# Merging the block inverses of both halves of a DeltaNet head together, with one set of decays

## The chip, the cores and the metric

The kernel runs on one core of one Trainium2 chip. The metric is the device time of one execution in microseconds (us). TensorE, VectorE, ScalarE, GpSimd and SyncE appear in the profile as PE, DVE, ACT, POOL and SP; PEld is the load of stationary operands into TensorE, SPq the queue in which SP issues transfers.

## The reference: what is computed

One layer of a decoder with two head groups, for a prompt of 2048 tokens and for 8 single-token samples. The part that matters here is the gated DeltaNet group (4 heads of width 128), computed chunk by chunk:

```python
G = jnp.cumsum(gc, axis=-1)
diff = G[..., :, None] - G[..., None, :]
L = jnp.exp(jnp.where(causal, diff, -jnp.inf))
kb = kc * bc[..., None]
A = jnp.where(strict, jnp.einsum('bhtk,bhsk->bhts', kb, kc) * L, 0.0) + eye
rhs = jnp.concatenate([vc * bc[..., None], kb * jnp.exp(G)[..., None]], axis=-1)
sol = lax.linalg.triangular_solve(A, rhs, left_side=True, lower=True, unit_diagonal=True)
u = sol[..., :V] - jnp.einsum('bhtk,bhkv->bhtv', sol[..., V:], s)
attn = jnp.einsum('bhtk,bhsk->bhts', qc, kc) * L
o = (jnp.einsum('bhtk,bhkv->bhtv', qc * jnp.exp(G)[..., None], s)
     + jnp.einsum('bhts,bhsv->bhtv', attn, u))
```

Around it stand an input projection of width 4104, an HGRN2 group of the same size, gates, norms, and an output projection of 1024 by 1024 with a residual and a final norm.

## The kernel before, in words

The prompt is worked in two groups of 1024 tokens (`g`), each in two halves of 512 tokens (`sb`, four chunks of 128). For each group the four heads follow one another, so there are eight (group, head) pairs, called heads below. Projections run as three products of split operands (`xh`, `xl`, `wh`, `wl`) into `ps_pj`. The recurrences of the heads run as generators beside them. Every operation is recorded by `Engine` (line 392 in all rows; TensorE's products are on line 505, its transposes on line 512), and `Model.plan` sets the order on each engine by a list schedule with a table of costs (`_time`, and `hold` in `mm`). The engines then run that order, so an engine whose next instruction is not ready waits even if a later one is.

For one DeltaNet head:

- `decays` makes, for each half, two masked sets of decays from the gates' cumulated logs: `la` (rows t, columns s, mask `mnA`) and `lt` (rows s, columns t, mask `mnT`), four scalar_tensor_tensor and one Exp each.
- `gk_after` and `gq_after` make the scalars `gam`, `nge`, `br`, the products `ps_kq` of keys with keys and queries, `la` = products times `gam` times `la`, `lt` = products times `lt`. The 32 by 32 diagonal blocks of `la` go through DRAM (`ad`) into `xa`, one block a partition.
- `substitute` inverts all 32 blocks of a head (both halves) at once on DVE: 31 steps of two operations, `tm<-xa,ti` and `ti<-ti,tm`. The result goes through DRAM (`td`) into the diagonal blocks of `ut`, one tile per half, eight transfers a head.
- `inverse`, one generator per half, merges blocks of 32 into 64 and 64 into 128: four groups of small products (`ps_v1`, `ps_u1`, `ps_v2`, `ps_u2`; the profile shows them as `ps_v` and `ps_u` with 32 or 64 columns), each followed by copies on DVE, and a 32 by 32 block transpose of `ut` into `tn`.
- `gdn_chain` walks the chunks: `ps_ks`, `rr`, `ps_u<-rr,ut`, `uu`, `ps_s`, the state `s_gd`, and the output `po_g`.

After the eighth head's projections the output projection (`ps_y`) begins, while the last head's substitution, merge and chain still run.

Of the kernel before, what the change touches and what calls it, by code (L numbers as in the profile page):

```python
# [7 lines left out]
F32 = mybir.dt.float32  # L8
# [9 lines left out]
P = 128  # L18
# [385 lines left out]
def build(tc, x_prompt, x_sample, state_hgrn, state_gdn, state_gdn_conv, norm_w, w_in, hg_lb_logits,  # L404
# [10 lines left out]
    with ctx:  # L415
# [79 lines left out]
        def until(cond):  # L495
            while not cond():
                yield 0.3
# [206 lines left out]
        def gates_post(g, gt, out):  # L704
# [127 lines left out]
        def gk_after(g, h, sb, gt):  # L832
            cs = slice(sb * 4, sb * 4 + 4)

            def run(u):
                yield from until(lambda: "ek" in u)
                ps = yield from tr4(r4(u[1]), "ps_k")
                ss = sumsq4(ps, "ssk")
                V.tensor_scalar(ss, ss, 4 * EPS, None, op0=ALU.add)
                rk = small.tile([P, 4], F32, tag="rk", name="rk")  # L840
                rsqrt(rk, ss)
                kn = keep.tile([P, 4, P], F32, tag="kn", name="kn")
                V.tensor_tensor(kn, ps, bc4(u["ek"]), op=ALU.mult)
                u["kn"] = kn
                yield
                br = small.tile([P, 4], F32, tag="br", bufs=6, name="br")
# [34 lines left out]

        def gq_after(sb, U):
            def run(u):
# [8 lines left out]
                k2, q2 = r4(u[1]), r4(u[0])  # L892
                la, lt, gam = u["la"], u["lt"], u["gam"]
                for c2 in range(2):
# [6 lines left out]
                    for c in range(2):  # L901
                        cc = 2 * c2 + c
                        V.scalar_tensor_tensor(la[:, cc], in0=pk[:, c, 0], scalar=gam[:, cc:cc + 1], in1=la[:, cc], op0=ALU.mult, op1=ALU.mult)
                    V.tensor_tensor(lt[:, 2 * c2:2 * c2 + 2], pk[:, :, 1], lt[:, 2 * c2:2 * c2 + 2], op=ALU.mult)
                for b in range(4):
                    Q.dma_start(U["ad"][b, sb * 4:sb * 4 + 4].rearrange("c t s -> t c s"),
                                      la[32 * b:32 * b + 32, :, 32 * b:32 * b + 32])
# [12 lines left out]
        def substitute(U):  # L920
# [3 lines left out]
            for cg in range(4):  # L924
                Q.dma_start(xa[32 * cg:32 * cg + 32], U["ad"].rearrange("b c t s -> (b c) t s"))
            ti = dec.tile([P, 8, 32], F32, tag="ti", name="ti")
# [16 lines left out]
            for sb in range(NSB):  # L943
                ut = keep.tile([P, 4, P], F32, tag="ut", name="ut")
                G.memset(ut, 0.0)
                for b in range(4):
                    Q.dma_start(ut[32 * b:32 * b + 32, :, 32 * b:32 * b + 32],
                                      td[b, sb * 4:sb * 4 + 4].rearrange("c s t -> s c t"))
                U[sb]["ut0"] = ut
            for sb in range(NSB):  # L950
                start(inverse(U[sb], sb), 0)

        def inverse(u, sb):
            la, ut = u["la"], u["ut0"]
            v1, v2 = v12[sb]
# [3 lines left out]
            yield from ready(la, ut, slot=CH)  # L959
            pv = ch.tile([P, 4, 32], F32, tag="ch", name="ps_v1")  # L960
            for c in range(4):
                for q in (0, 64):
                    mm(pv[q:q + 32, c], lhsT=la[:, c, q:q + 32], rhs=ut[:, c, q + 32:q + 64], start=True, stop=True)
            for q in (0, 64):
                V.tensor_copy(v1[q:q + 32], pv[q:q + 32])
            yield from ready(v1, tn, slot=CH)
            pu = ch.tile([P, 4, 32], F32, tag="ch", name="ps_u1")
            for c in range(4):
                for q in (0, 64):
                    mm(pu[q:q + 32, c], lhsT=tn[:, c, q:q + 32], rhs=v1[:, c], start=True, stop=True)  # L970
                mm(pu[32:64, c], lhsT=v1[:, c], rhs=tn[:, c, 0:32], start=True, stop=True)
            for q in (0, 64):
                V.tensor_scalar(ut[q:q + 32, :, q + 32:q + 64], pu[q:q + 32], -1.0, None, op0=ALU.mult)
            V.tensor_scalar(tn[32:64, :, 0:32], pu[32:64], -1.0, None, op0=ALU.mult)
            yield from ready(ut, slot=CH)
            pv2 = ch.tile([P, 4, 64], F32, tag="ch", name="ps_v2")
            for c in range(4):
                mm(pv2[:64, c], lhsT=la[:, c, 0:64], rhs=ut[:, c, 64:128], start=True, stop=True)
            V.tensor_copy(v2[0:64], pv2[:64])
            yield from ready(v2, tn, slot=CH)  # L980
            pu2 = ch.tile([P, 4, 64], F32, tag="ch", name="ps_u2")
            for c in range(4):
                mm(pu2[:64, c], lhsT=tn[:, c, 0:64], rhs=v2[:, c], start=True, stop=True)
            opened[0] -= 1
            V.tensor_scalar(ut[0:64, :, 64:128], pu2[:64], -1.0, None, op0=ALU.mult)
            u["ut"] = ut

        def gdn_chain(g, h, U, gt):
            S = s_gd[h]
            for sb in range(NSB):  # L990
# [6 lines left out]
                for c in range(4):  # L997
# [506 lines left out]
        for i, (g, h, off, sb, part) in enumerate(steps):  # L1504
# [6 lines left out]
            if i == 7:  # L1511
# [5 lines left out]
                G.affine_select(out=mnT, in_=mnT, compare_op=ALU.is_ge, fill=NEG, base=0, pattern=[[1, P]], channel_multiplier=-1)  # L1517
                mnA = ctile([P, P], "mnA")
                G.memset(mnA, 0.0)
                G.affine_select(out=mnA, in_=mnA, compare_op=ALU.is_gt, fill=NEG, base=0, pattern=[[-1, P]], channel_multiplier=1)  # L1520
                t0 = ctile([P, 8, 32], "t0")
# [6 lines left out]
                for b in range(2):  # L1528
                    G.memset(scT[b], 0.0)
                v12 = [(ctile([P, 4, 32], f"v1{b}"), ctile([P, 4, 64], f"v2{b}")) for b in range(2)]  # L1530
                for t in v12:
                    G.memset(t[0], 0.0)
                    G.memset(t[1], 0.0)
                zpad = ctile([P, NS, 40], "zpad")
# [28 lines left out]
            elif off == GQ:  # L1563
                post = conv_post(0, h, UG[sb], gq_after(sb, UG), lambda u=UG[sb]: "gam" in u)
            elif off == GV:
# [265 lines left out]
```

## Time and profile before

| what | before |
|---|---|
| time, median of 3 runs (lowest, highest) | 1274.28 us (1273.73, 1276.13) |
| the profiled execution: its own time | 1279.08 us |
| the profiled execution: span from first to last instruction | 1277.3 us |
| PE busy | 1220.3 us, 96% of the span |
| DVE busy | 950.4 us, 74% |
| ACT busy | 519.1 us, 41% |
| POOL busy | 306.3 us, 24% |

Busy time is the time in which an engine executed something. A product of four-byte floats shows as two rows per instruction on PE, and rows of PE overlap, since its products are pipelined: the duration of a row is longer than its distance to the next one.

### The profile page before, as it was taken

Reading aid. Unit: us, or ns where it says so; the run is one execution under the profiler, and the core shown is the slowest. Engines: PE = TensorE matmul, PEld = TensorE weight load, DVE = VectorE, ACT = ScalarE, POOL = GpSimd, SP = SyncE. Lnnn points to the kernel's source line nnn. Section 1 sums busy time; section 2 is a strip of 40 time slices with the busy share of each in tenths; the row PEclk is TensorE's granted clock in tenths of the full one; section 3 lists DMA queues with packets and bytes.
Section 4 is the critical chain, followed back from the end, with each engine's and each line's share of the span. In section 5 each row is a group of like instructions: output and inputs, shape, how many; then the busy total and the mean of one; then the engine's idle time right before and its main releaser. Section 6 shows DMA issues by size and latency. Waiting matters only on the chain.

```text
span 1277.3 us, 21956 instructions
## 1 busy us (share of the span) xinstructions
PE 1220.3 (96%) x7943; PEld 1056.3 (83%) x7943; DVE 950.4 (74%) x2419; ACT 519.1 (41%) x1533; POOL 306.3 (24%) x304
## 2 busy tenths in 40 slices
PE   3999999999999999989999999999999999999997
PEld 3988898988898889987788878888887887877785
DVE  4467897689876986888788987896788677954433
ACT  5435523643264325653365326423622464222221
POOL 5221321332232322322224213221322220001000
PEclk9999999999999999999999999999999999999998
DMA  5222532332333321334144432221332216442442
GB/s 177 66 50 85 80 41 58 71 100 64 79 93 86 92 58 42 87 108 111 34 118 57 65 68 69 70 56 30 80 76 49 68 49 202 129 144 83 144 144 82
DMA packets 144053, 107.52 MB, mean 84 GB/s; under 512 B 26122, under 2 KB 126792, under 8 KB 143928
## 3 DMA queue, kind: packets, MB, share of 16 engines
q1 hardware_dynamic: 143936, 106.02, 32.8%
q8 instruction: 65, 1.06, 0.3%
q14 instruction: 52, 0.43, 0.1%
HBM read 82.23 MB, written 23.91 MB: 83 GB/s over the span
## 4 chain that ended last, share of the span: by engine, by line
PE 69%; DVE 15%; DMA 9%; SPq 3%; issue 2%; ACT 1%; POOL 0%; POOLq 0%; DVEq 0%; ACTq 0%
PE ps_pj L505 35%; PE ps_y L505 14%; DVE tm L392 4%; DVE ti L392 4%; SPq L392 3%; PE ps_u L505 2%; PE po_h L505 2%; PE po_g L505 2%; PE ps_kq L505 2%; DMA ut<-td 2%; DMA xt<-in_x_prompt_dram 1%; DVE E L392 1%; PE ps_g L505 1%; PE ps_ks L505 1%; PE ps_hu L505 1%
## 5 line engine op out<-in xcount | busy, mean ns | idle before, releaser
L505 PE MATMUL ps_pj<-xh,wh 128*128 128x512 f32 (+2 forms) x1328 | 469.8, 354 | 7.9 <-ACT pre L392 2.7
L505 PE MATMUL ps_pj<-xh,wl 128*128 128x512 f32 (+2 forms) x1328 | 466.2, 351 | 0.0
L505 PE MATMUL ps_pj<-xl,wh 128*128 128x512 f32 (+2 forms) x1328 | 465.2, 351 | 0.2 <-DVE xl L392 0.2
L505 PEld LDWEIGHTS ps_pj<-xh,wh 128*128 128x128 f32 x1328 | 253.4, 191 | 34.8 <-ACT pre L392 3.3
L505 PEld LDWEIGHTS ps_pj<-xl,wh 128*128 128x128 f32 x1328 | 253.5, 191 | 24.2 <-DVE xl L392 0.5
L505 PEld LDWEIGHTS ps_pj<-xh,wl 128*128 128x128 f32 x1328 | 253.4, 191 | 24.3
L392 POOL TENSOR_TENSOR wl<-raw,wh 128x512 fp32r<-128x512 f32 x128 | 172.9, 1352 | 359.6 <-ACT wh L392 319.9
L392 ACT ACTIVATE wh<-raw 128x512 fp32r<-128x512 f32 x128 | 80.5, 629 | 158.4 <-PE ps_pj L505 111.3
L392 DVE TENSOR_TENSOR tm<-xa,ti 128x248 f32<-128x248 f32 (+30 forms) x248 | 107.5, 434 | 14.6 <-DMA xa<-ad 9.4
L505 PE MATMUL ps_y<-woh,oh 128*128 128x512 f32 x256 | 101.4, 400 | 4.9 <-ACT oh L392 3.0
L505 PE MATMUL ps_y<-woh,ol 128*128 128x512 f32 x256 | 101.0, 396 | 0.0
L505 PE MATMUL ps_y<-wol,oh 128*128 128x512 f32 x256 | 100.4, 394 | 0.0
L392 DVE TENSOR_TENSOR ti<-ti,tm 128x248 f32<-128x248 f32 (+30 forms) x248 | 90.4, 365 | 7.5
L392 ACT ACTIVATE jk<-xt 128x512 bf16<-128x512 f32 (+2 forms) x54 | 40.0, 740 | 121.9 <-DVE xt L392 88.2
L392 POOL TENSOR_TENSOR rso<-sso,mhalf 128x4 f32<-128x4 f32 x32 | 35.8, 1119 | 115.7 <-DVE sso L392 111.5
L505 PEld LDWEIGHTS ps_y<-woh,oh 128*128 128x128 f32 x256 | 48.5, 190 | 15.1 <-ACT oh L392 3.5
L392 POOL TENSOR_TENSOR frs<-fss,mhalf 128x1 f32<-128x1 f32 (+1 forms) x17 | 9.5, 557 | 198.4 <-DVE fss L392 180.9
L505 PEld LDWEIGHTS ps_y<-woh,ol 128*128 128x128 f32 x256 | 48.4, 189 | 10.3 <-DVE ol L392 0.4
L505 PEld LDWEIGHTS ps_y<-wol,oh 128*128 128x128 f32 x256 | 48.6, 190 | 9.4
L392 DVE TENSOR_TENSOR xt<-ps_y,xt 128x512 f32<-128x512 f32 (+1 forms) x34 | 23.4, 688 | 39.4 <-PE ps_y L505 38.0
L392 ACT ACTIVATE s_hg<-s_hg,e 128x128 f32<-128x128 f32 x80 | 32.0, 400 | 43.0 <-DVE s_hg L392 32.3
L392 DVE SCALAR_TENSOR_TENSOR s_gd<-s_gd,el,ps_s 128x128 f32<-128x128 f32 x64 | 22.1, 346 | 30.8 <-PE ps_s L505 30.3
(290 smaller groups left out, 2169.5 us busy)
## 6 DMA issues: line engine op xcount, KB each, us to landing
raw<-in_w_in_dram SPq DMA_DIRECT2D x128, 256.0 KB
xt<-in_x_prompt_dram SPq DMA_DIRECT2D x30, 512.0 KB
og_d<-sz SPq DMA_DIRECT2D x32, 256.0 KB
og<-og_d SPq DMA_DIRECT2D x32, 256.0 KB
out_dram<-xt SPq DMA_DIRECT2D x15, 512.0 KB
gb<-gate_r SPq DMA_DIRECT2D x16, 256.0 KB
out_dram<-S SPq DMA_DIRECT2D x8, 512.0 KB
xa<-ad SPq DMA_DIRECT2D x32, 128.0 KB
```

What stands on the lines that cost most here:

```text
L392: r = fn(*args, **kw)
L505: r = T.matmul(out, lhsT=lhsT, rhs=rhs, start=start, stop=stop)
```

## The change

Three things change together.

First, the merge runs once for a head instead of once for each half. `ut` becomes one tile of eight chunks with one buffer (before: two buffers of four chunks), filled by four transfers of eight blocks instead of eight of four. The products, their number and their sizes stay: per head 16 for `ps_v1`, 24 for `ps_u1`, 8 each for `ps_v2` and `ps_u2`. They now read the transposed blocks first (`tn`, and the new `tq` for columns 64 to 95), so both block transposes stand ahead of the first product. The 64-column products of even and odd chunks write partitions 0 to 63 and 64 to 127 of a PSUM tile in turn; before, all wrote partitions 0 to 63. Copies out of PSUM hold eight chunks.

Second, the diagonal `gam` is no longer folded into the rows of the matrix that is inverted, but into its columns, so `la` can be made from `lt`, and the set with mask `mnA` goes away. The factor comes back in `uu`, which becomes a scaled copy out of PSUM, and `br` and `nge` lose it.

Third, `ad` holds the blocks the other way round, and `tm` reads `xa` along its last axis instead of with a step of 32 elements.

```diff
             eG = small.tile([P, NH, 8], F32, tag="eG", bufs=2, name="eG")
             A.activation(eG, Gc, AF.Exp)
+            V.tensor_scalar(eG, eG, -1.0, None, op0=ALU.mult)
...
-                V.tensor_tensor(br, rk, gt["beta"][:, h, cs], op=ALU.mult)
-                gam = small.tile([P, 4], F32, tag="gam", bufs=6, name="gam")
-                V.tensor_tensor(gam, br, rk, op=ALU.mult)
-                nge = small.tile([P, 4], F32, tag="nge", bufs=6, name="nge")
-                V.scalar_tensor_tensor(nge, in0=gam, scalar=-1.0, in1=gt["eG"][:, h, cs], op0=ALU.mult, op1=ALU.mult)
-                V.tensor_scalar(br, br, 0.5, None, op0=ALU.mult)
-                u["br"], u["nge"], u["gam"] = br, nge, gam
+                V.scalar_tensor_tensor(br, in0=ss, scalar=0.5, in1=rk, op0=ALU.mult, op1=ALU.mult)
+                u["br"], u["nge"], u["gam"] = br, gt["eG"][:, h, cs], gam
...
-            for key, after, mask in (("la", "ut", mnA), ("lt", "done", mnT)):
-                yield from until(lambda: after in prev)
-                lx = keep.tile([P, 4, P], F32, tag=key, name=key)
-                for c in range(4):
-                    gcol = gt["Gc"][:, h, sb * 4 + c:sb * 4 + c + 1]
-                    V.scalar_tensor_tensor(lx[:, c], in0=gb4[:, c], scalar=gcol, in1=mask, op0=ALU.subtract, op1=ALU.min, reverse0=(key == "la"))
-                    yield
-                A.activation(lx, lx, AF.Exp)
-                u[key] = lx
+            yield from until(lambda: "done" in prev)
+            lt = keep.tile([P, 4, P], F32, tag="lt", name="lt")
+            for c in range(4):
+                gcol = gt["Gc"][:, h, sb * 4 + c:sb * 4 + c + 1]
+                V.scalar_tensor_tensor(lt[:, c], in0=gb4[:, c], scalar=gcol, in1=mnT, op0=ALU.subtract, op1=ALU.min)
+                yield
+            A.activation(lt, lt, AF.Exp)
+            u["lt"] = lt
...
-                        V.scalar_tensor_tensor(la[:, cc], in0=pk[:, c, 0], scalar=gam[:, cc:cc + 1], in1=la[:, cc], op0=ALU.mult, op1=ALU.mult)
+                        V.scalar_tensor_tensor(la[:, cc], in0=pk[:, c, 0], scalar=gam[:, cc:cc + 1], in1=lt[:, cc], op0=ALU.mult, op1=ALU.mult)
...
-                SE.tensor_tensor(tm[:, :, :n], xa[:, j + 1:, j].unsqueeze(1).broadcast_to(sh),
+                SE.tensor_tensor(tm[:, :, :n], xa[:, j, j + 1:].unsqueeze(1).broadcast_to(sh),
...
-            for sb in range(NSB):
-                ut = keep.tile([P, 4, P], F32, tag="ut", name="ut")
-                G.memset(ut, 0.0)
-                for b in range(4):
-                    Q.dma_start(ut[32 * b:32 * b + 32, :, 32 * b:32 * b + 32],
-                                      td[b, sb * 4:sb * 4 + 4].rearrange("c s t -> s c t"))
+            ut = keep.tile([P, 8, P], F32, tag="ut", bufs=1, name="ut")
+            G.memset(ut, 0.0)
+            for b in range(4):
+                Q.dma_start(ut[32 * b:32 * b + 32, :, 32 * b:32 * b + 32], td[b].rearrange("c s t -> s c t"))
+            start(inverse(U, ut), 0)
...
-            tn = btile([P, 4, P], "tn", F32)
-            V.transpose(tn.rearrange("p c k -> p (c k)"), ut.rearrange("p c k -> p (c k)"))
+            tn = btile([P, 8, 64], "tn", F32)
+            tq = dec.tile([P, 8, 32], F32, tag="tm", name="tq")
+            V.transpose(tn, ut[:, :, 0:64])
+            V.transpose(tq, ut[:, :, 64:96])
...
-            for c in range(4):
-                mm(pv2[:64, c], lhsT=la[:, c, 0:64], rhs=ut[:, c, 64:128], start=True, stop=True)
-            V.tensor_copy(v2[0:64], pv2[:64])
+            for c in range(8):
+                q = 64 * (c % 2)
+                mm(pv2[q:q + 64, c // 2], lhsT=la(c)[:, 64:128], rhs=tn[:, c], start=True, stop=True)
+            for q in range(2):
+                V.tensor_copy(v2[64:128, q::2], pv2[64 * q:64 * q + 64])
...
-                    A.copy(uu, p2)
+                    A.activation(uu, p2, AF.Copy, scale=u["gam"][:, c:c + 1])
```

The order on every engine is planned anew, so instructions move all through the program. Two places show the pattern.

PE at the first head's merge, before (`ps_v_2389` and `ps_v_2415` are the first products of the two halves, `ps_u_2449` and `ps_u_2465` the second ones, `ps_v_2493` and `ps_v_2501` the third):

```order
L505 MATMUL ps_sc<-E,kp 128x128 x2
L505 MATMUL ps_v_2389<-ut,la 32x32 x8
L505 MATMUL ps_v_2415<-ut,la 32x32 x8
L505 MATMUL ps_sc<-E,kp 128x128 x2
L505 MATMUL ps_pj<-xh,wl 128x512
...
L505 MATMUL po_h<-vn,scT_702 128x128
L505 MATMUL ps_v_2493<-ut,la 64x64 x4
L505 MATMUL po_h<-s_hg_102,E 128x128
L505 MATMUL ps_v_2501<-ut,la 64x64 x4
L505 MATMUL ps_u_2509<-v_707,tn 64x64 x4
L505 MATMUL ps_pj<-xh,wh 128x512
```

The same place on PE in the changed kernel, in two pieces, the start of the first group and the last two groups:

```order
L505 MATMUL ps_pj<-xl,wh 128x512
L505 MATMUL ps_v_2376<-tn,la 32x32
L505 MATMUL ps_pj<-xh,wl 128x512
L505 MATMUL ps_v_2376<-tq,la 32x32
...
L505 MATMUL ps_v_2455<-tn,la 64x64 x8
L505 MATMUL ps_pj<-xl,wh 128x512
L505 MATMUL ps_pj<-xh,wl 128x512
L505 MATMUL ps_pj<-xh,wh 128x512
L505 MATMUL ps_u_2480<-ut,v_702 64x64 x8
L505 MATMUL po_h<-vn,scT_697 128x128
```

The two halves' groups have become one group each, and the first products now read the transposed blocks. Over the whole program the small products stand in 52 unbroken stretches before and in 37 after.

DVE at the same place, before: each half has its own transpose, and the copies of the second group of products follow.

```order
L392 TENSOR_TENSOR E<-ps_pj,E 128x256
L392 STREAM_TRANSPOSE tn<-ut 128x512
L392 COPY el<-gb 128x4
L392 SCALAR_TENSOR_TENSOR smp<-t_1321,smp 128x8
L392 STREAM_TRANSPOSE tn<-ut 128x512
L392 SCALAR_TENSOR_TENSOR smp<-t_1456,smp 128x8
L392 COPY v_706<-ps_v_2389 32x128 x2
L392 COPY v_708<-ps_v_2415 32x128 x2
```

DVE there in the changed kernel:

```order
L392 TENSOR_SCALAR ssq<-ssq 128x4
L392 STREAM_TRANSPOSE tn<-ut 128x512
L392 STREAM_TRANSPOSE tq<-ut 128x256
L392 TENSOR_TENSOR E<-ps_pj,E 128x256
L392 SCALAR_TENSOR_TENSOR smp<-t_1742,smp 128x8
L392 TENSOR_SCALAR fs<-ks,lbc 128x8
L392 TENSOR_SCALAR ks<-ks,lbc 128x8
L392 TENSOR_TENSOR ek<-gb,Gc 128x4 x2
L392 COPY carry<-pre 128x3
L392 COPY zpad<-smp 128x8
L392 COPY v_701<-ps_v_2376 32x256 x2
```

Both transposes stand together, in front of PE's first product, and one pair of copies serves both halves.

## Rows read from the trace of the kernel before

**Rows 1.** The page's head: busy us, share of the span and instructions of each engine.

```profile
PE 1220.3 (96%) x7943; PEld 1056.3 (83%) x7943; DVE 950.4 (74%) x2419; ACT 519.1 (41%) x1533; POOL 306.3 (24%) x304
```

**Rows 2.** PE's waits over the span: us in total, times, longest.

```profile
PE ps_v L505 <- DMA ut<-td: 7.7, 9, 2.6
...
PE ps_u L505 <- DVE v L392: 1.6, 2, 0.9
```

**Rows 3.** Timeline of PE, first merge: start, us, what, count, [idle before].

```profile
198.79 0.45 PE L505 MATMUL ps_v<-ut,la 128*32 128x32 f32 x16
199.66 0.25 PE L505 MATMUL ps_v<-ut,la 128*32 128x32 f32 x2 [0.43 <-DMA ut<-td]
201.97 0.44 PE L505 MATMUL ps_v<-ut,la 128*32 128x32 f32 x14 [2.06 <-DMA ut<-td]
```

**Rows 4.** Stretches: length, busy of PE, PEld, DVE, ACT, POOL, then granted clock.

```profile
202.34:205.70 3.36, 3.36 (x59) 2.61 (x55) 2.81 (x13) 0.20 (x1) 0.00 (x0) 0.50 0.36 126
...
602.40:609.00 6.60, 6.60 (x52) 4.66 (x53) 5.54 (x11) 0.33 (x1) 0.00 (x0) 0.54 0.03 6
```

**Rows 5.** Timeline of PE, one 64-column group of the second head.

```profile
347.55 0.28 PE L505 MATMUL ps_pj<-xl,wh 128*128 128x256 f32 x1
347.67 0.28 PE L505 MATMUL ps_pj<-xh,wl 128*128 128x256 f32 x1
...
347.90 0.39 PE L505 MATMUL ps_hu<-vn,ktn 128*128 128x128 f32 x2
348.22 0.68 PE L505 MATMUL ps_v<-ut,la 128*64 128x64 f32 x8
348.83 0.39 PE L505 MATMUL ps_pj<-xl,wh 128*128 128x256 f32 x1
349.05 0.39 PE L505 MATMUL po_g<-uu,lt 128*128 128x128 f32 x2
349.27 0.39 PE L505 MATMUL po_g<-s_gd,qp 128*128 128x128 f32 x2
```

**Rows 6.** Groups of PE by form: count, busy us, mean ns of one.

```profile
L505 PE MATMUL ps_v<-ut,la 128*64 128x64 f32 x128 | 10.5, 227 | 1.7 <-issue 1.1 <-PE ps_u L505 0.7
L505 PE MATMUL ps_v<-ut,la 128*32 128x32 f32 x256 | 9.6, 202 | 7.8 <-DMA ut<-td 7.7
```

**Rows 7.** Groups of DVE: count, busy us, mean ns of one, idle before.

```profile
L392 DVE TENSOR_TENSOR tm<-xa,ti 128x248 f32<-128x248 f32 (+30 forms) x248 | 107.5, 434 | 14.6 <-DMA xa<-ad 9.4
L392 DVE TENSOR_TENSOR ti<-ti,tm 128x248 f32<-128x248 f32 (+30 forms) x248 | 90.4, 365 | 7.5
...
L392 DVE SCALAR_TENSOR_TENSOR la<-gb,Gc,mnA 128x128 f32<-128x128 f32 x64 | 19.7, 342 | 0.0
...
L392 DVE STREAM_TRANSPOSE tn<-ut 128x512 f32<-128x512 f32 x16 | 11.4, 710 | 22.3 <-DMA ut<-td 22.1
```

**Rows 8.** Groups of ACT, in the same columns.

```profile
L392 ACT ACTIVATE wh<-raw 128x512 fp32r<-128x512 f32 x128 | 80.5, 629 | 158.4 <-PE ps_pj L505 111.3 <-issue 29.8 <-DMA raw<-in_w_in_dram 12.3
...
L392 ACT COPY uu<-ps_u 128x128 f32<-128x128 f32 x64 | 16.9, 264 | 55.7 <-PE ps_u L505 55.1
...
L392 ACT ACTIVATE k<-pre,cols 128x512 f32<-128x512 f32 x16 | 11.5, 721 | 5.2 <-PE ps_ks L505 5.2
...
L392 ACT ACTIVATE la<-la 128x512 f32<-128x512 f32 x16 | 10.0, 625 | 10.0 <-DVE la L392 5.6 <-PE ps_hu L505 4.4
```

**Rows 9.** Timeline of SP, first head.

```profile
195.60 3.64 SPq L392 DMA_DIRECT2D ut<-td  x8
```

**Rows 10.** The chain that ended last, around the same place: start, us, what.

```profile
198.81 3.11 DMA ut<-td
```

**Rows 11.** All that touches `ut` in the second head: count, ns, first and last start.

```profile
L505 PE MATMUL ps_u<-rr,ut x16: 270/275/275, 342.5 to 375.3; 128*128 128x128 f32 x16
...
L392 POOL MEMSET ut<- x2: 525/526/528, 357.0 to 375.6; 128x512 f32 x2
```

**Rows 12.** All that touches `ut` at the third head: count, ns, first and last start.

```profile
L392 SPq DMA_DIRECT2D ut<-td x8: 316/432/433, 464.3 to 467.5; - x8
```

More of the change, by code (lines that the diff above doesn't have):

```diff
@@ L845, in run @@
                 yield
+                gam = small.tile([P, 4], F32, tag="gam", bufs=6, name="gam")
+                V.tensor_tensor(gam, rk, gt["beta"][:, h, cs], op=ALU.mult)
+                V.tensor_tensor(gam, gam, rk, op=ALU.mult)
                 br = small.tile([P, 4], F32, tag="br", bufs=6, name="br")
-                V.tensor_tensor(br, rk, gt["beta"][:, h, cs], op=ALU.mult)
-                gam = small.tile([P, 4], F32, tag="gam", bufs=6, name="gam")
-                V.tensor_tensor(gam, br, rk, op=ALU.mult)
-                nge = small.tile([P, 4], F32, tag="nge", bufs=6, name="nge")
-                V.scalar_tensor_tensor(nge, in0=gam, scalar=-1.0, in1=gt["eG"][:, h, cs], op0=ALU.mult, op1=ALU.mult)
-                V.tensor_scalar(br, br, 0.5, None, op0=ALU.mult)
-                u["br"], u["nge"], u["gam"] = br, nge, gam
+                V.scalar_tensor_tensor(br, in0=ss, scalar=0.5, in1=rk, op0=ALU.mult, op1=ALU.mult)
+                u["br"], u["nge"], u["gam"] = br, gt["eG"][:, h, cs], gam
             return run
@@ L880, in decays, with gq_after @@
             u.update(eb=gb, el=el)
-        def gq_after(sb, U):
+        def gq_after(sb, U, prev):
             def run(u):
@@ L892, in run @@
                 k2, q2 = r4(u[1]), r4(u[0])
-                la, lt, gam = u["la"], u["lt"], u["gam"]
+                yield from until(lambda: "ut" in prev)
+                la = u["la"] = keep.tile([P, 4, P], F32, tag="la", name="la")
+                lt, gam = u["lt"], u["gam"]
                 for c2 in range(2):
@@ L902, in run @@
                         cc = 2 * c2 + c
-                        V.scalar_tensor_tensor(la[:, cc], in0=pk[:, c, 0], scalar=gam[:, cc:cc + 1], in1=la[:, cc], op0=ALU.mult, op1=ALU.mult)
+                        V.scalar_tensor_tensor(la[:, cc], in0=pk[:, c, 0], scalar=gam[:, cc:cc + 1], in1=lt[:, cc], op0=ALU.mult, op1=ALU.mult)
                     V.tensor_tensor(lt[:, 2 * c2:2 * c2 + 2], pk[:, :, 1], lt[:, 2 * c2:2 * c2 + 2], op=ALU.mult)
                 for b in range(4):
-                    Q.dma_start(U["ad"][b, sb * 4:sb * 4 + 4].rearrange("c t s -> t c s"),
+                    Q.dma_start(U["ad"][b, sb * 4:sb * 4 + 4].rearrange("c s t -> s c t"),
                                       la[32 * b:32 * b + 32, :, 32 * b:32 * b + 32])
@@ L924, in substitute @@
             for cg in range(4):
-                Q.dma_start(xa[32 * cg:32 * cg + 32], U["ad"].rearrange("b c t s -> (b c) t s"))
+                Q.dma_start(xa[32 * cg:32 * cg + 32], U["ad"].rearrange("b c s t -> (b c) s t"))
             ti = dec.tile([P, 8, 32], F32, tag="ti", name="ti")
@@ L950, in substitute @@
[L950 to L955, printed above, removed]
-            yield from hold()
-            tn = btile([P, 4, P], "tn", F32)
-            V.transpose(tn.rearrange("p c k -> p (c k)"), ut.rearrange("p c k -> p (c k)"))
-            yield from ready(la, ut, slot=CH)
-            pv = ch.tile([P, 4, 32], F32, tag="ch", name="ps_v1")
-            for c in range(4):
-                for q in (0, 64):
[L963 to L971, printed above, removed]
+            ut = keep.tile([P, 8, P], F32, tag="ut", bufs=1, name="ut")
@@ new lines, in substitute, with inverse, la @@
+            G.memset(ut, 0.0)
+            for b in range(4):
+                Q.dma_start(ut[32 * b:32 * b + 32, :, 32 * b:32 * b + 32], td[b].rearrange("c s t -> s c t"))
+            start(inverse(U, ut), 0)
+        def inverse(U, ut):
+            def la(c):
+                return U[c // 4]["la"][:, c % 4]
+            yield from hold()
+            tn = btile([P, 8, 64], "tn", F32)
+            tq = dec.tile([P, 8, 32], F32, tag="tm", name="tq")
+            V.transpose(tn, ut[:, :, 0:64])
+            V.transpose(tq, ut[:, :, 64:96])
+            yield from ready(U[1]["la"], tn, tq, slot=CH)
+            pv = ch.tile([P, 8, 32], F32, tag="ch", name="ps_v1")
+            for c in range(8):
+                mm(pv[0:32, c], lhsT=la(c)[:, 32:64], rhs=tn[:, c, 0:32], start=True, stop=True)
+                mm(pv[64:96, c], lhsT=la(c)[:, 96:128], rhs=tq[:, c], start=True, stop=True)
+            for q in (0, 64):
+                V.tensor_copy(v1[q + 32:q + 64], pv[q:q + 32])
+            yield from ready(v1, ut, slot=CH)
+            pu = ch.tile([P, 8, 32], F32, tag="ch", name="ps_u1")
+            for c in range(8):
+                for q in (0, 64):
+                    mm(pu[q:q + 32, c], lhsT=v1[:, c], rhs=ut[:, c, q + 32:q + 64], start=True, stop=True)
+                mm(pu[32:64, c], lhsT=ut[:, c, 32:64], rhs=v1[:, c], start=True, stop=True)
+            V.tensor_scalar(tn[32:64, :, 0:32], pu[32:64], -1.0, None, op0=ALU.mult)
@@ L972, in inverse @@
             for q in (0, 64):
                 V.tensor_scalar(ut[q:q + 32, :, q + 32:q + 64], pu[q:q + 32], -1.0, None, op0=ALU.mult)
-            V.tensor_scalar(tn[32:64, :, 0:32], pu[32:64], -1.0, None, op0=ALU.mult)
-            yield from ready(ut, slot=CH)
+            yield from ready(tn, slot=CH)
             pv2 = ch.tile([P, 4, 64], F32, tag="ch", name="ps_v2")
-            for c in range(4):
-                mm(pv2[:64, c], lhsT=la[:, c, 0:64], rhs=ut[:, c, 64:128], start=True, stop=True)
@@ L979, in inverse @@
-            V.tensor_copy(v2[0:64], pv2[:64])
-            yield from ready(v2, tn, slot=CH)
-            pu2 = ch.tile([P, 4, 64], F32, tag="ch", name="ps_u2")
[L982 to L986, printed above, removed]
+            for c in range(8):
+                q = 64 * (c % 2)
+                mm(pv2[q:q + 64, c // 2], lhsT=la(c)[:, 64:128], rhs=tn[:, c], start=True, stop=True)
@@ new lines, in inverse @@
+            opened[0] -= 1
+            for q in range(2):
+                V.tensor_copy(v2[64:128, q::2], pv2[64 * q:64 * q + 64])
+            yield from ready(v2, ut, slot=CH)
+            pu2 = ch.tile([P, 4, 64], F32, tag="ch", name="ps_u2")
+            for c in range(8):
+                q = 64 * (c % 2)
+                mm(pu2[q:q + 64, c // 2], lhsT=v2[:, c], rhs=ut[:, c, 64:128], start=True, stop=True)
+            for q in range(2):
+                V.tensor_scalar(ut[0:64, q::2, 64:128], pu2[64 * q:64 * q + 64], -1.0, None, op0=ALU.mult)
@@ L988, in gdn_chain @@
+            for sb in range(NSB):
+                U[sb]["ut"] = ut[:, 4 * sb:4 * sb + 4]
         def gdn_chain(g, h, U, gt):
@@ L1517, in build @@
                 G.affine_select(out=mnT, in_=mnT, compare_op=ALU.is_ge, fill=NEG, base=0, pattern=[[1, P]], channel_multiplier=-1)
-                mnA = ctile([P, P], "mnA")
-                G.memset(mnA, 0.0)
-                G.affine_select(out=mnA, in_=mnA, compare_op=ALU.is_gt, fill=NEG, base=0, pattern=[[-1, P]], channel_multiplier=1)
                 t0 = ctile([P, 8, 32], "t0")
@@ L1529, in build @@
                     G.memset(scT[b], 0.0)
[L1530 to L1533, printed above, removed]
+                v1, v2 = ctile([P, 8, 32], "v1"), ctile([P, 8, 64], "v2")
+                G.memset(v1, 0.0)
+                G.memset(v2, 0.0)
                 zpad = ctile([P, NS, 40], "zpad")
@@ L1563, in build @@
             elif off == GQ:
-                post = conv_post(0, h, UG[sb], gq_after(sb, UG), lambda u=UG[sb]: "gam" in u)
+                post = conv_post(0, h, UG[sb], gq_after(sb, UG, prev_g[sb]), lambda u=UG[sb]: "gam" in u)
             elif off == GV:
```

1 line of the change is left out of this document (removed).

## The prediction

> **What bounds the kernel now.** I read the page's head first: TensorE executes something in 1220.3 of 1277.3 us, DVE in 950.4 [rows 1]. So time is won only where PE needs fewer cycles or waits less; work taken from DVE or ACT counts only if PE was waiting for it. The changed products are a small part of PE's work but stand in an awkward place: four times a head PE does a handful of narrow products, DVE copies them out, and PE's next group needs the copies.
>
> PE's waits name this place after the start-up: 7.7 us for the transfer `ut<-td`, 1.6 us for the copies `v` [rows 2], and 1.8 us more before `ps_v` [rows 6]; 11.1 us in all. The timeline of the first merge shows one of them: eight products of the second half, of which the first can start at 199.66, and the rest 2.06 us later, when the transfer lands [rows 3]. Behind that wait the granted clock is 0.50 of full (1.2 instead of 2.4 GHz) for 3.36 us, and behind a like wait in the fourth head 0.54 for 6.60 us [rows 4]. That is work lost of 3.36 x 0.50 + 6.60 x 0.46 = 4.7 us. So the merges' stalls cost 15.8 us.
>
> **A, the 64-column products.** Their number stays at 128 instructions, 256 rows on PE: 128 rows of `ps_v` [rows 6] and as many of `ps_u`. Eight rows take 0.68 us from first start to last end and one lasts 0.227 [rows 5, 6], so the distance is (0.68 - 0.23)/7 = 0.065 us; the first distance is longer than the rest, so I take 0.058. The change makes neighbours write different halves of PSUM's partitions. What that does is shown by the 32-column products, which alternate between partitions 0 and 64 already: 16 rows in 0.45 us [rows 3], (0.45 - 0.20)/15 = 0.017 us a row, where half of 0.058 would be 0.029. Two of them share the array. If the 64-column ones share it too, 256 x 0.058/2 = **7.4 us** go; if not, nothing. I take 7.4, since the 32-column rows also use all 128 partitions of input and differ only in width.
>
> A rule speaks against this. By the Trainium skill, TensorE: Matmul & The Clock Gate, section "The mechanism" of Part 3, a weight load overlaps products in flight only when the row group differs, and here all rows are used by both neighbours; by it A would be 0. The trace disagrees for the 32-column products (0.017 us a row with all 128 rows in use); no row shows it for 64 columns.
>
> **B, entering and leaving the narrow products.** In the second head `ps_hu` starts at 347.90, and `po_g` behind the group at 349.05 [rows 5]: 1.15 us. Of it two rows of `ps_hu` take 0.22 (as 349.05 to 349.27), one 256-column product 0.12 (as 347.55 to 347.67), eight narrow rows 0.47. The rest, 0.34 us, is the price of a stretch. The program's order has 52 stretches before and 37 after: 15 x 0.34 = **5.1 us** less. Bounds: 3 (if stretches that follow each other closely already share a price) and 5.1.
>
> **C, the stalls of the merges.** For less: `tm` takes 107.5 us and `ti` with the same sizes 90.4 [rows 7], so reading `xa` with a step costs up to 17.1 us, 2.1 a head, in a serial chain of 62 operations that PE ends up waiting for. If the step is the cause (`tm` also has broadcast inputs, which `ti` has not, so the rows can't tell), `ut` is ready 2.1 us earlier. The kernel's table of costs gives `tm` and `ti` the same price, so the planned order was early by that much, and this error goes. Four fewer issues of `ut<-td` give 3.64/2 = 1.8 us [rows 9], if the queue and not the blocks sets the landing. Eight `la` operations a head, 19.7 us in all [rows 7], leave DVE.
>
> For more: PE's first product needs all of `ut` and a transpose of 0.71 us, and the second a further one of about half that [rows 7]; before, it read `ut` as it landed, and the first half could start while the second half was on its way. The landing behind the last issue took 3.11 us [rows 10] for the same bytes. In the first head a transfer `gb<-gate_r` now stands between `td` and `ut` on SP's queue.
>
> Bounds: all stalls gone, -15.8; or in each of the eight heads a wait of 2.06 [rows 3] plus both transposes, 1.07, plus a lost 3.36 x 0.50 = 1.68: 8 x 4.81 = 38.5, which is 22.7 more than now. Earlier data by some 2 us against a later first product by some 1 us speaks for the better side, but not for its end: **5 us** less.
>
> **D, what is hidden.** ACT loses 16 `la` Exps, 10.0 us, and its 64 `uu` copies become scaled ones. A scaled pass over 512 columns takes 721 ns, a plain one 629 [rows 8]; 64 x 0.092 = 5.9 us more on the states' chain. PE does projections in that time, and `ps_s`, which needs `uu`, does not stand among its waits: 0, and +5.9 if that cover fails, which is least likely before the last head. On DVE, besides `la`: one and a half transposes of the old size a head instead of two save about 16 x 0.71/4 = 2.8 us, fewer but longer copies about 5, small scalars about 2; together some 29 of 950 us, from an engine that is idle for 327. Outside the merges I take 0. The single buffer of `ut`: in the second head the last product that reads it starts at 375.3 and the memset follows at 375.6 [rows 11], while the third head's transfers into it begin at 464.3 [rows 12]. 88 us cover the longer memset; without them it would cost about 0.5 us a head.
>
> **E, the new plan.** All engines are ordered anew, so waits elsewhere (start-up, the change of token group) move by chance; 0, within 5 us either way.
>
> **Sum.** 7.4 + 5.1 + 5 = 17.5 us. The profiled execution took 1279.08 us, 1.8 more than its span and 4.8 more than the median of the three runs; 1279.08 - 17.5 = 1261.6, and against the median 1274.28 - 17.5 = 1256.8. I predict **1257 us**, 1.4% faster. About 0.2% (2.5 us) is what a measurement of this kernel can tell from no change.
>
> **Rivals.**
>
> 1. *The merge waits for both halves* (slower). One landing, two transposes and four longer copies now stand in one chain with no other half to fill in. If every head stalls as in the upper bound of C, 22.7 us are lost against 12.5 won by A and B: 1274.3 + 10.2 = 1284.5. It decides from stalls of (15.8 + 12.5)/8 = 3.5 us a head on, half clock included. For it: the planned order puts PE's first product where the table of costs expects the landing, and the trace shows landings later than what PE had been ordered to do. Against: `tm` has become what the table says.
> 2. *The 64-column products don't share the array.* The rows stay 0.058 us apart as those of one half of the partitions do now, so A is 0: 1257 + 7.4 = 1264. For it: no row of before has two 64-column products side by side. Against: the 32-column rows. The rule of the Trainium skill named under A would give this case.
> 3. *PE gives it back.* PE arrives earlier at its next wait, for a projection's evacuation or a transfer, and the waits that were short grow: 1270 to 1277, say 1273. For it: DVE is busy for 74% of the span. Against: PE had no more than some 11 us of waits at the merges and is busy for 96%.
> 4. *The stalls go altogether*: 7.4 + 5.1 + 15.8 = 28.3, 1246 us.
>
> **How the numbers follow.** The forecast has 0.53 (its own range 1250 to 1262), rival 1 0.11, rival 2 0.13, rival 3 0.11, rival 4 0.12. The predicted time is the forecast's. The range 1243 to 1274 takes in rivals 2 and 4 and most of rival 3, with E's 3 us below rival 4; rival 1 and the far end of 3 stay out. Faster by over 0.2%: 0.53 + 0.13 + 0.12 and about 0.04 of rival 3, 0.82. Slower: 0.09, most of rival 1. The same: 0.09, the rest of both.
>
> **What the next profile would show.** A: eight pairs of 64-column rows with the two rows of a pair some 10 ns apart, and about 0.03 us a row; 0.058 refutes it. B: 37 stretches at about 0.34 us. C: PE's waits at the first product, now for DVE's `tn`, of less than 11 us in all, and no slices at half clock behind them; `tm` with 240 elements as long as `ti`. D: `uu` near 0.36 us. The prediction is wrong if PE's waits for `tn` come to more than 3 us a head, or if the waits at start-up and at the change of token group grow by more than the merges win.

## The result and the profile after

| | before | after |
|---|---|---|
| median of the runs shown with the result (lowest, highest) | 1274.01 us (1269.41, 1276.13) | 1257.16 us (1255.99, 1258.65) |
| the profiled execution: its own time | 1279.08 us | 1258.65 us |
| the profiled execution: span | 1277.3 us | 1256.9 us |

The ratio of after to before is 0.9883, with a 95% interval of 0.9856 to 0.991: 1.2% faster. The two profiles lie 20.4 us apart and the medians 16.9, because the profiled execution of before was 5 us above its median and that of after 1.5 us.

The page's head of the changed kernel (busy us, share of the span, instructions):

```profile
PE 1206.1 (96%) x7943; PEld 1041.1 (83%) x7943; DVE 903.2 (72%) x2301; ACT 513.7 (41%) x1517; POOL 302.8 (24%) x292
```

PE executes the same 7943 instructions in 14 us less [rows 1]; DVE has lost 47 us, and what those are worth is tested below (e2, m1, e3). PE's waits in the changed kernel (us in total, times, longest):

```profile
PE ps_x L512 <- DVE xt L392: 19.8, 6, 16.0
...
PE ps_u L505 <- DVE v L392: 1.5, 2, 1.3
PE ps_v L505 <- DVE tn L392: 1.3, 1, 1.3
PE ps_v L505 <- DVE ut L392: 1.1, 2, 0.7
```

The 7.7 us for `ut<-td` [rows 2] are gone, and no wait for the two transposes took their place: ahead of the first products PE waits less than 0.1 us at a time. The 1.3 us under `tn` are a single wait ahead of the third products of the fourth head, for the copy `tn<-ps_u` that stands on DVE behind a reciprocal. PE there, and DVE:

```profile
597.11 0.69 PE L505 MATMUL ps_v<-tn,la 128*64 128x64 f32 x16 [1.34 <-DVE tn L392]
```

```profile
594.87 1.75 DVE L392 RECIPROCAL E<-E 128x256 f32<-128x256 f32 x1
596.64 0.42 DVE L392 TENSOR_SCALAR tn<-ps_u 32x256 f32<-32x256 f32 x1
```

The last 64-column groups of the program, from PE's timeline (start, us, what, count):

```profile
1122.38 0.39 PE L505 MATMUL ps_y<-woh,oh 128*128 128x512 f32 x1
1122.70 0.69 PE L505 MATMUL ps_v<-tn,la 128*64 128x64 f32 x16
1123.32 0.50 PE L505 MATMUL ps_y<-wol,oh 128*128 128x512 f32 x1
1123.65 0.40 PE L505 MATMUL ps_y<-woh,ol 128*128 128x512 f32 x1
```

Sixteen rows take what eight took [rows 5]: (0.69 - 0.23)/15 = 0.031 us a row. The groups of PE, DVE and ACT that answer to rows 6 to 8 (count, busy us, mean ns, idle before):

```profile
L505 PE MATMUL ps_u<-ut,v 128*64 128x64 f32 x128 | 6.5, 241 | 0.0
L505 PE MATMUL ps_v<-tn,la 128*64 128x64 f32 x128 | 5.5, 228 | 2.4 <-DVE tn L392 1.3 <-DVE ut L392 1.1
```

```profile
L392 DVE TENSOR_TENSOR ti<-ti,tm 128x248 f32<-128x248 f32 (+30 forms) x248 | 91.8, 370 | 7.7
L392 DVE TENSOR_TENSOR tm<-xa,ti 128x248 f32<-128x248 f32 (+30 forms) x248 | 85.3, 344 | 19.3 <-DMA xa<-ad 14.7
...
L392 DVE STREAM_TRANSPOSE tn<-ut 128x512 f32<-128x512 f32 x8 | 5.7, 707 | 3.1 <-DMA ut<-td 3.1
```

```profile
L392 ACT ACTIVATE uu<-ps_u,gam 128x128 f32<-128x128 f32 x64 | 23.3, 365 | 64.5 <-PE ps_u L505 63.7
```

One long stretch at half clock is left beside the program's start and end, in the fourth head's merge behind that wait (columns as in rows 4, then DMA share and GB/s):

```profile
598.20:605.02 6.82, 6.31 (x33) 4.35 (x34) 6.04 (x14) 0.00 (x0) 0.72 (x1) 0.50 0.12 29
```

**An account of the small products.** For each stretch of `ps_v` and `ps_u` products (32 and 64 columns) I took from PE's rows the time from the start of the product ahead of it to the start of the second product behind it, less what the two wide products need among their like (0.227 us for 512 columns, 0.12 for 256, 0.11 a row for 128). The group above gives 1123.65 - 1122.38 - 0.45 = 0.82 us: 0.46 for its rows (from first start to last) and some 0.35 for its edges, where the forecast had 0.34. Summed over the program this is **60.0 us before and 36.8 after**. Without stalls the eight heads' merges would have rows of 8.1 us (32 columns), of 14.6 before or 7.4 after (64 columns: 32 groups of 0.457, or 16 of 0.464), and 0.34 a stretch. Taken off, the stalls inside merges remain: 60.0 - 22.7 - 52 x 0.34 = 19.6 before, 36.8 - 15.5 - 37 x 0.34 = 8.7 after. The 23.2 us less split into 7.2 for the rows (A), 5.1 for 15 fewer stretches (B) and 10.9 for stalls (C); the span fell by 20.4, so 2.8 came back elsewhere. B is the count of stretches times the forecast's own price, not a measurement by itself; C is what is left.

### The profile page after: what moved, and what is told of

Read it like the earlier page. It is cut to its first block, busy times and chain, and to the rows that moved or that the text cites. A ratio compares the mean times of both kernels' runs of the same rounds, so it can differ in the third digit from the quotient of the medians.

```text
span 1256.9 us, 21690 instructions
## 1 busy us (share of the span) xinstructions
PE 1206.1 (96%) x7943; PEld 1041.1 (83%) x7943; DVE 903.2 (72%) x2301; ACT 513.7 (41%) x1517; POOL 302.8 (24%) x292
## 4 chain that ended last, share of the span: by engine, by line
PE 48%; DMA 3%; DVE 2%; issue 1%; ACT 1%; SPq 0%; POOL 0%; POOLq 0%; DVEq 0%; ACTq 0%
PE ps_pj L505 23%; PE ps_y L505 14%; DMA wor<-in_w_out_dram 1%; PE po_g L505 1%; PE ps_u L505 1%; PE ps_kq L505 1%; PE po_h L505 1%; PE ps_ks L505 1%; PE ps_s L505 1%; DMA raw<-in_w_in_dram 1%; PE ps_sc L505 1%; PE ps_o L512 1%; PE ps_g L505 1%; PE ps_hu L505 1%; SPq L392 0%
## 5 line engine op out<-in xcount | busy, mean ns | idle before, releaser
L392 POOL TENSOR_TENSOR wl<-raw,wh 128x512 fp32r<-128x512 f32 x128 | 169.8, 1327 | 363.6 <-ACT wh L392 338.7
L392 DVE TENSOR_TENSOR tm<-xa,ti 128x248 f32<-128x248 f32 (+30 forms) x248 | 85.3, 344 | 19.3 <-DMA xa<-ad 14.7
L392 ACT ACTIVATE uu<-ps_u,gam 128x128 f32<-128x128 f32 x64 | 23.3, 365 | 64.5 <-PE ps_u L505 63.7
```

The lines of the kernel that those rows point to most:

```text
L392: r = fn(*args, **kw)
```

## The experiments

Each is timed against the kernel before on the same chip. The last three columns are that account of each profiled execution. e0, e1 and e3 have the same order on every engine; all other runs are planned anew.

| run | median us | ratio to before, 95% interval | small products | stretches | stalls in them |
|---|---|---|---|---|---|
| e0_after | 1255.71 | 0.9888 (0.9867, 0.9909) | 36.8 | 37 | 8.7 |
| e1_one_side | 1259.08 | 0.9919 (0.9899, 0.9939) | 42.1 | 37 | 6.8 |
| e2_halves | 1272.31 | 1.0013 (0.9995, 1.003) | 51.9 | 48 | 12.9 |
| e3_step | 1259.68 | 0.9919 (0.99, 0.9939) | 36.2 | 37 | 8.1 |
| m1_two_sets | 1258.80 | 0.9897 (0.9866, 0.9928) | 37.6 | 36 | 9.9 |
| e4_eight | 1267.45 | 0.9944 (0.9921, 0.9966) | 43.1 | 38 | 14.7 |
| c1_step_price | 1281.59 | 1.0061 (1.0038, 1.0083) | 60.0 | 53 | 19.3 |
| p_before_045 | 1271.23 | 1.0002 (0.9984, 1.002) | 55.8 | 46 | 17.5 |
| p_after_045 | 1251.62 | 0.9844 (0.9814, 0.9874) | 34.8 | 36 | 7.1 |
| p_before_070 | 1276.84 | 1.0033 (1.0012, 1.0053) | 64.8 | 52 | 24.4 |
| p_after_070 | 1257.67 | 0.9853 (0.982, 0.9886) | 34.9 | 37 | 6.8 |
| i1_prices | 1251.48 | 0.9842 (0.9808, 0.9875) | 33.0 | 35 | 5.6 |

Beside them before had medians of 1270.78 (first four rows), 1270.11 (the two with 045, m1, i1) and 1272.37 us (e4, c1, the two with 070).

**e0_after**, the changed kernel as it is, as the yardstick.

> The changed kernel once more, as the yardstick for the runs beside it: 1255 to 1260 us, 1.1 to 1.3% faster than before.

The gain came again, at 1.1%.

**e1_one_side** takes the alternating partitions away; the order on every engine stays. The PSUM tile becomes twice as long, and the copies out of it read it with a step, which doesn't lengthen them (413 ns against 423).

```diff
-                mm(pv2[q:q + 64, c // 2], lhsT=la(c)[:, 64:128], rhs=tn[:, c], start=True, stop=True)
+                mm(pv2[0:64, c], lhsT=la(c)[:, 64:128], rhs=tn[:, c], start=True, stop=True)
...
-                mm(pu2[q:q + 64, c // 2], lhsT=v2[:, c], rhs=ut[:, c, 64:128], start=True, stop=True)
+                mm(pu2[0:64, c], lhsT=v2[:, c], rhs=ut[:, c, 64:128], start=True, stop=True)
```

> The changed kernel with all 64-column products writing partitions 0 to 63 of a full PSUM bank, as in the kernel before; the order on every engine stays word for word. If neighbours on different partitions share the array (term A), a group of 16 rows goes back from 0.46 to about 0.93 us between its first and last start, and the time rises by 8 x 2 x 0.46 = 7.4 us, to about 1264.5. If PE's saved time was given back at its next wait, the groups grow but the time rises by less than 3 us. If they never shared, nothing changes.

PE's timeline of this kernel, at the group shown above:

```profile
1121.79 0.40 PE L505 MATMUL ps_y<-woh,oh 128*128 128x512 f32 x1
1122.11 1.15 PE L505 MATMUL ps_v<-tn,la 128*64 128x64 f32 x16
1123.19 0.50 PE L505 MATMUL ps_y<-wol,oh 128*128 128x512 f32 x1
1123.53 0.39 PE L505 MATMUL ps_y<-woh,ol 128*128 128x512 f32 x1
```

The same sixteen rows need (1.15 - 0.23)/15 = 0.061 us each instead of 0.031. So in this kernel two products that write different halves of PSUM's partitions do share the array; whether the array's columns or PSUM's partitions decide it can't be told apart here. The small products take 5.3 us more than in e0, and the time is 0.3% (4 us) longer, about as much as the intervals can tell apart, and between the 7.4 us of full value and the 3 us of a gain given back: the stalls fell by 1.9 us, so part of what the pairs win on PE it waits away.

**e2_halves** merges each half by itself again, with its own `ut`, four transfers a half, and 64-column products on partitions 0 to 63; the one set of decays, the diagonal in the columns, the transposes ahead of the first product and the unit step of `tm` stay.

```diff
-            ut = keep.tile([P, 8, P], F32, tag="ut", bufs=1, name="ut")
...
-                Q.dma_start(ut[32 * b:32 * b + 32, :, 32 * b:32 * b + 32], td[b].rearrange("c s t -> s c t"))
-            start(inverse(U, ut), 0)
+            for sb in range(NSB):
+                ut = keep.tile([P, 4, P], F32, tag="ut", name="ut")
...
+            for sb in range(NSB):
+                start(inverse(U[sb], sb), 0)
```

> The changed kernel with the merge once per half again (four chunks a tile, two ut tiles, eight transfers a head, 64-column products all on partitions 0 to 63), while the single set of decays, the diagonal on the columns and the unit-step reads of xa stay. If the merge itself (A and B) brought the gain, 7.4 us come back and some 15 stretches at 0.34 us another 5: 1268 to 1272. If the gain came from DVE's shorter substitution and fewer decays, it stays within 4 us of the changed kernel.

No difference to before that can be measured, and 0.3 us above the range that was expected if the merge makes the gain: in this order, everything but the joint merge brings nothing by itself. The stalls of its profile are 6.7 us below those of before, but the profiled execution of before was itself 5 us above its median, so part of that may belong to that execution.

**m1_two_sets** keeps the joint merge and gives `la` a set of decays of its own again: 64 more scalar_tensor_tensor on DVE and 16 more Exps on ACT.

```diff
+            for key, after in (("la", "ut"), ("lt", "done")):
...
+                A.activation(lx, lx, AF.Exp)
+                u[key] = lx
```

> The changed kernel with two sets of decays again: la gets its own four masked operations and Exp per half, 64 DVE and 16 ACT instructions more (the mask is that of lt, so the result stays that of the reference); the merge, the sharing of the array and the unit step stay. If the merge gives the gain, 1256 to 1260 us, within 4 us of the changed kernel. If the relief of DVE is a condition of it, 1262 to 1270 us.

Its time lies in the range expected if the merge makes the gain, and its ratio and that of e0 lie 0.1% apart, within both intervals. The set of decays that the change saves is worth nothing that these runs can see.

**e3_step** gives `tm` its step of 32 elements back, in the same order of all engines. The blocks still lie the other way round, so it multiplies by the elements across each block's diagonal, and its inverses are not those of the reference.

```diff
-                SE.tensor_tensor(tm[:, :, :n], xa[:, j, j + 1:].unsqueeze(1).broadcast_to(sh),
+                SE.tensor_tensor(tm[:, :, :n], xa[:, j + 1:, j].unsqueeze(1).broadcast_to(sh),
```

> The changed kernel, with tm reading xa with a step of 32 elements again (it then reads the wrong half of each block, so the inverses are not those of the reference); the order on every engine stays word for word. If the step costs DVE time, tm goes from 85 to about 107 us in all, 2.7 us a head. If PE's merges wait for the substitution (term C), that shows as new waits before ps_v and half clock behind them: 8 to 25 us more, 1265 to 1282. If the substitution has slack in the planned order, less than 3 us.

Groups of DVE in e3_step:

```profile
L392 DVE TENSOR_TENSOR tm<-xa,ti 128x248 f32<-128x248 f32 (+30 forms) x248 | 110.7, 446 | 19.5 <-DMA xa<-ad 14.9
L392 DVE TENSOR_TENSOR ti<-ti,tm 128x248 f32<-128x248 f32 (+30 forms) x248 | 91.8, 370 | 7.7
```

The step does cost DVE 25 us, 3.2 a head, in one chain. The time grew by 0.3% (4 us, again at the edge of the intervals, and between the two expectations), but not at the merges: their stalls are 8.1 us, as in e0 (8.7). So the step is the cause of the longer `tm`, and the joint merges don't stall for it. For the two half merges this run doesn't show that; there the unit step stands only in e2, beside other changes, with stalls of 12.9 us.

**c1_step_price** tests the other half of C's first reason, the planner's price, in the kernel before: the planner is told what the stepped `tm` costs.

```diff
+        if any(a.tensor.name.startswith("xa") for a in ins):
+            return 0.155 + 0.00182 * n, 0.0, True
```

> The kernel before, with one number changed: the planner's table gives tm (which reads xa with a step) 0.155 us + 0.00182 us an element instead of the price of ti, so that the planned order puts the merges as late as DVE really reaches them. Theory (the old merges stalled because the order was early by the table's error): PE's waits for the transfer ut<-td fall below 3 us (7.7 before), and the time falls by 4 to 8 us, 1263 to 1267. Rival (the stalls come from the shape of the two half merges, and a later order only makes other waits): within 3 us of before, with narrow stretches that still sum to over 54 us (60.4 in the profile of before).

PE's waits of c1_step_price:

```profile
PE ps_v L507 <- DMA ut<-td: 7.2, 7, 3.0
```

Both sides missed. The kernel became 0.6% slower, PE still waits 7.2 us for the transfers, and the stalls are the same 19 us. In this one order a right price for `tm` does not place the old merges better.

**e4_eight** fills the joint `ut` with eight transfers again, each of four blocks.

```diff
-                Q.dma_start(ut[32 * b:32 * b + 32, :, 32 * b:32 * b + 32], td[b].rearrange("c s t -> s c t"))
+                for sb in range(NSB):
+                    Q.dma_start(ut[32 * b:32 * b + 32, 4 * sb:4 * sb + 4, 32 * b:32 * b + 32], td[b, 4 * sb:4 * sb + 4].rearrange("c s t -> s c t"))
```

> The changed kernel with ut filled by eight transfers of four blocks again instead of four of eight. Theory (the queue's four extra issues, 1.8 us a head, delay the first product, but the order expects them): 0 to 2 us slower than the changed kernel, 1256 to 1258, and PE waits for the transposes tn of under 4 us. Rival (the number of issues is what emptied the merges of stalls): 6 us slower or more, with waits of 1 us or more at the first product in several heads.

It is 0.56% (7 us) slower than e0 by the ratios, whose intervals don't touch, far above what the queue alone was given, and the stalls rise from 8.7 to 14.7 us. That is the time of the rival that was written down, but not its place: only one head waits 1 us or more at its first product. The largest wait stands ahead of the second products of the first merge. SP, then DVE, then PE there (timelines of e4_eight):

```profile
194.87 3.64 SPq L392 DMA_DIRECT2D ut<-td  x8
198.61 0.39 SPq L392 DMA_DIRECT2D raw<-in_w_in_dram  x1
199.09 0.92 SPq L392 DMA_DIRECT2D gb<-gate_r  x2
```

```profile
204.43 0.16 DVE L392 TENSOR_TENSOR ek<-gb,Gc 128x4 f32<-128x4 f32 x1 [3.62 <-DMA gb<-gate_r]
...
205.28 0.85 DVE L392 COPY v<-ps_v 32x256 f32<-32x256 f32 x2
```

```profile
206.18 0.27 PE L505 MATMUL ps_u<-ut,v 128*32 128x32 f32 x2 [3.78 <-DVE v L392]
```

PE waits for the copies `v`; they stand on DVE behind `ek`, which waits for `gb`; and `gb` stands on SP's queue behind the eight issues of `ut<-td`. In e0 four issues took 1.79 us, one `gb` had gone ahead of them, and PE waited 1.17 us at this place (SP, then PE):

```profile
197.33 0.34 SPq L392 DMA_DIRECT2D gb<-gate_r  x1
197.84 1.79 SPq L392 DMA_DIRECT2D ut<-td  x4
```

```profile
205.97 0.22 PE L505 MATMUL ps_u<-ut,v 128*32 128x32 f32 x2 [1.17 <-DVE v L392]
```

Half clock follows the longer wait, and not the shorter one (windows of e4_eight and of e0_after, columns as above):

```profile
206.03:209.44 3.41, 3.26 (x59) 2.45 (x61) 1.35 (x4) 0.00 (x0) 1.27 (x1) 0.51 0.20 31
```

```profile
205.97:209.38 3.41, 3.33 (x76) 2.50 (x78) 3.08 (x10) 0.55 (x1) 0.00 (x0) 1.00 0.00 0
```

With 3.41 x 0.49 = 1.7 us lost there, the first merge accounts for 3.78 - 1.17 + 1.7 = 4.3 of the 6.0 us. The order of this kernel is a new one too, and that no `gb` went ahead of the issues is the order's doing, so a part may be chance. The five orders with four transfers (e0, m1 and three more below) lie at ratios of 0.9842 to 0.9897, all below e4's 0.9944, which is about half way to before.

**p_before_045, p_after_045, p_before_070, p_after_070** plan both kernels with another fixed latency for each dependence, which makes other orders of the same work.

```diff
-        return took + 0.055
+        return took + 0.045
```

> The kernel before with one number of its planner changed (0.045 instead of 0.055 us between an instruction's end and one on another engine that needs it), so that the order of all engines is another one and the work is the same. If the order's chance matters little (term E within 5 us), 1266 to 1276 us, still above every kernel with the merge. If the measured gain is mainly a luckier order, this spreads by 10 us or more.

> The changed kernel with the same number of the planner changed. If the merge itself gives the gain, it stays 12 to 20 us faster than its counterpart of before: 1250 to 1261 us. If the order's chance gave it, 1262 us or more.

> The kernel before, planned with a fixed latency of 0.070 us a dependence instead of 0.055: another order of the same work. It shows how much an order alone is worth. If orders scatter by some 5 us, 1266 to 1276; if the old order was an unlucky one, under 1264.

> The changed kernel planned with 0.070 us instead of 0.055: another order of the same work. If the gain belongs to the merge and not to the one order, 12 to 20 us faster than the kernel before with the same 0.070; if a lucky order made it, less than 8.

At 0.045 the change is worth 1271.23 - 1251.62 = 19.6 us, at 0.070 1276.84 - 1257.67 = 19.2, at the kernels' own 0.055 1270.78 - 1255.71 = 15.1 (e0). p_before_070 ended just above its range. So the gain isn't that of one lucky order: every order of the old kernel has a ratio of 1 to 1.0061 (c1), every one of the new with four transfers 0.9842 to 0.9897. An order alone moves the time by up to 0.6% (8 us) in the old kernel and 0.5% (6 us) in the new.

**i1_prices** gives the planner of the changed kernel the distances that its rows show for the small products.

```diff
+            if lhsT.dtype != F32R and n <= 64 and k <= 64:
+                hold = 0.061 if k == 64 else 0.0213 if "ps_u1" in out.tensor.name else 0.032
```

> The changed kernel with the planner's prices of the merge's products set to what the trace shows: 0.061 us for a 64-column product that shares the array, 0.032 and 0.021 for the 32-column ones (before 0.116 and 0.05). If the saving of the sharing is partly given back because the order still keeps their old room, 2 to 4 us faster than the changed kernel: 1252 to 1255 us. If not, within 3 us of it.

It is the fastest with p_after_045, 0.46% below e0 (4.2 us by the medians, just beyond the 2 to 4 that were expected), and has the least stalls, 5.6 us. As another latency brings the same, better prices can't be told from another order.

## Why the prediction was right

The forecast was 1257 us; 1257.16 were measured, and 17.5 us less against 16.9. Its terms were right in kind, C only in part, and its errors cancelled; that they did so to less than a microsecond is luck.

**A, right.** 7.4 us forecast, 7.2 found on PE (rows of 0.031 us); e1 shows that the alternation makes them. In time it is worth some 4 us, since PE waits a little more when it needs less time for its products. Rival 2 is refuted: neighbours that write different halves of the partitions need 0.031 us a row, those that write the same half 0.061. The rule of the Trainium skill, TensorE: Matmul & The Clock Gate, section "The mechanism" of Part 3, by which A would be 0, doesn't hold for these products, all of which use 128 rows of the array.

**B, right by the account.** 37 stretches, with edges of 0.35 us where nothing waits. No run changes their number alone, so the 5.1 us are not shown by themselves. The Trainium skill, TensorEngine Tiling (Array Packing), section "Key Properties", says that a change of the tiling mode drains the engine, without a price; the trace agrees that entering and leaving costs something, 0.34 to 0.35 us here.

**C, right in sign, mis-sized, and its first reason not borne out.** 5 us forecast, 10.9 found between the two profiles. How much of that is the slow profiled execution of before is open; but the pair at 0.045, whose old kernel was profiled 1.6 us above its median, has 17.5 - 7.1 = 10.4 as well, and the pair at 0.070 has 24.4 - 6.8 = 17.6. The first reason, `tm`'s step and its price in the table, found no support: the step costs more than was read from `ti` (3.2 us a head, not 2.1), but e3 has it and no more stalls, and c1 has the price and no fewer. The second, four fewer issues, was given 1.8 us a head on the queue alone; in e4 it goes with 6.0 us of stalls, because what stands behind the issues waits too (traced for the first merge, where the order has a part in it). That `gb` stood there was in the text; what waited for it was not followed. Against a later first product the prediction had set 1 us a head; PE, ordered to do other work in that time, waits for the transposes less than 0.1 us at a time. No slice at half clock was to be left behind the merges; one of 6.82 us stands in the fourth head's, behind a copy. What is left open is how much of 19.6 us in before belongs to the two half merges themselves and how much to its order: four orders of the old kernel give 17.5 to 24.4 us, e2 12.9, and the changed kernel with four transfers 5.6 to 9.9. e2 also has its transposes ahead of the first products, and whether that lowers its stalls no run shows.

**D, right.** `uu` takes 365 ns, 6.4 us more in all, and doesn't show among PE's waits with more than 0.8 us; the decays saved on DVE and ACT aren't missed either when they return (m1), and alone they bring nothing (e2).

**E and rival 3, small and real.** 2.8 us of the 23.2 came back between the two profiles, and likewise 21.0 - 17.9 = 3.1 in the pair at 0.045 and 29.9 - 22.6 = 7.3 at 0.070, so it recurs with other orders. All this although three half-clock stretches of 3.41 us outside the merges of before (at 417, 557 and 1076 us) have no counterpart after. It isn't the start-up, where PE is busy for 20.0 of the first 40 us in both kernels; at the change of token group PE's waits before `ps_x` grew from 1.7 to 3.3 us. Orders scatter by up to 8 us where 5 were allowed. Rival 1 (the merge waits for both halves) needed 3.5 us a head; 8.7 us stand there for eight. Rival 4 (no stalls) came within 5.6 us of its assumption in i1.

**What cancelled.** The sum was 17.5 us against the profiled execution's own 1279.08, and was then taken from the median. C brought 5.9 us more than its 5. Of that, 2.8 came back elsewhere, where E had 0, and 3.5 stand only between the profiled executions, which lie 20.4 us apart, and not between the medians, which lie 16.9 apart. A C of the right size alone would have given 1274.3 - 23.4 = 1251 us, too low. No other execution of before on record was as long as the profiled one: the longest of the 47 beside the experiments took 1277.35 us. Which of its stalls a typical execution lacks is not shown.

## What to carry to other kernels

Cost a small transfer by what stands behind its issues on the queue, and follow that to the engine that runs in order: four more issues of 0.45 us a head went with 7 us of the time. Where groups of narrow products can write different halves of PSUM's partitions in turn, let them (0.031 instead of 0.061 us a row here), and put them into fewer stretches; work that was saved on an engine with slack (64 operations of DVE here) brought nothing that could be measured. Before explaining a gain of 1%, plan both kernels in two other orders: here the order alone is worth half a per cent, and the profile of one execution was 0.4 per cent off its median.

## What the runs showed that was not expected

A step of 32 four-byte elements in an input of DVE lengthens an operation on 248 elements from 444 to 626 ns in the mean of eight, and from 417 to 612 in the median. The groups of DVE by form, for the first step of the chain, in e3_step and in the changed kernel:

```profile
L392 DVE TENSOR_TENSOR tm<-xa,ti 128x248 f32<-128x248 f32 x8 | 5.0, 626 | 14.9 <-DMA xa<-ad 14.9
```

```profile
L392 DVE TENSOR_TENSOR tm<-xa,ti 128x248 f32<-128x248 f32 x8 | 3.6, 444 | 14.7 <-DMA xa<-ad 14.7
```

Yet 25 us of such work, in a serial chain in front of the merges, cost 4 us, none of it there; and telling the planner the price of that operation made the old kernel 0.6% slower.

The means are above the medians because single operations of DVE last longer than their like. In the changed kernel 75 of them exceed the median of their form by more than 0.6 us, 72 us in all, and every one of the 75 overlaps an operation of POOL, while of all TENSOR_TENSOR of DVE a fifth do. That the two engines delay each other is not tested by any run here.
